# Turning beta, kappa and v of an RWKV chunk with whole-array transposes

## Chip, core and metric

The kernel runs on one NeuronCore of one Trainium2 chip. The metric is the device time of one launch in microseconds. All times below are from executions on the chip.

## The reference

One block of a hybrid model over 256 tokens of width 2048. The normalised input is projected once; four branches (a gated linear recurrence, an attention with forgetting, an SSD scan and an RWKV-7 scan) work on parts of the projection, each result is multiplied by its own weights and its own gate, the sum goes through `w_out`, and a feed-forward stage and a gated embedding stage follow. Only the RWKV scan is touched here. Cut to it:

```python
def step(state, inp):                       # state: heads x 64 (v) x 64 (k)
    r_t, w_t, k_t, v_t, kk_t, a_t = inp
    sa = einsum('bhvk,bhk->bhv', state, -kk_t)
    state = (state * w_t[:, :, None, :] + sa[..., None] * (kk_t * a_t)[:, :, None, :]
             + v_t[..., None] * k_t[:, :, None, :])
    return state, einsum('bhvk,bhk->bhv', state, r_t)
```

There are 8 heads of 64 channels. Everything is float32.

## The kernel before

**The main stream.** Most of the work is a long row of projections with weights from HBM. Each weight piece (`wr`, 512 KB) is loaded by a DMA on the SP queue, split by ScalarE into a rounded part (`wh`, L212) and by VectorE into the rest (`wl`, L213), and TensorE multiplies each part with activations that are split in the same way (`x`, or `sb` and others), into PSUM tiles `pg` (pool `psG`, 4 banks). In the profile these are the rows `pg<-x,wh`, `pg<-x,wl` and `pg<-sb,wh` of L132. There are 4 buffers for `wr` and 3 each for `wh` and `wl`.

**The branches beside it.** Each branch is a generator (`lru`, `ssd`, `fox`, `rwkv`). After each few matmuls of a projection the function `pump` may run one step of the branch at the head of the list, up to its next `yield`; a small credit (`RATE` 0.5 for each call, at least `STEP` 0.2 spent for each step) keeps it from running ahead. Instructions of a branch have a lower priority than the main stream, but its TensorE instructions get the place of the main stream's current one plus `DELAY` (16) (`on_pe`, recorded as L135). From this a planner, which works with a simulated time, writes down one order of instructions for each engine, and each engine executes its own in order. The branches' PSUM tiles are `pb` (pool `psB`, 4 banks, taken with `bank()`). The order of the merge is: recurrence, SSD, attention, RWKV; the RWKV result is needed only when its own product with `w_branch` begins, after all the gates of its turn.

**RWKV.** The 256 tokens are four chunks of 64, and the heads stand in four pairs `j`: two heads share the 128 partitions, head h in partitions 64h to 64h+63 (`H2[h]`). For each chunk `c` a DMA brings `jc`, of shape [128 partitions, 4 pairs, 8 kinds, 64], in a buffer `e`. The kinds that matter here are 1 (beta), 2 (kappa) and 3 (v); in memory they are neighbours, 64 columns each, with kind 0 before kind 1. The partitions of kinds 1 to 3 are channels and their columns tokens; the products of the scan need them with tokens in the partitions. So three "turns" stand at the head of a chunk: `vc`, `btk` and `ktk` (the last two only for chunks 0 to 2, since the last chunk hands on no state).

A turn is `heads([(jc[:, :, k], ident)])`: for each pair and each head, a 64x64 block is turned into its place of a PSUM bank. Head 0 uses TensorE's transpose; head 1, whose block lies in partitions 64 to 127, is multiplied by the unit matrix `ident`, which lies in the constants `cbr`. `kept` then copies the 128x256 result to SBUF with ScalarE (L956). In the profile the rows of the turns on TensorE are `pb<-cbr,e`. After the turns come `uu`, `sa`, the new state `pS` and the output `py`, products of 64x64 blocks by the same `heads`. A `yield` stands behind each turn.

Lines that matter: 132 and 135 (the calls that record a matmul of the main stream and of a branch), 172 (`bank`), 937 to 951 (`heads`), 953 to 959 (`kept`), 960 to 966 (the turns), 968 to 986 (the rest of a chunk).

Of the kernel before, what the change touches and what calls it, by code (L numbers as in the profile page):

```python
# [14 lines left out]
P = 128  # L15
# [70 lines left out]
def body(tc, T, out, dbg=None):  # L86
    nc = tc.nc
    V, A, G, PE = nc.vector, nc.scalar, nc.gpsimd, nc.tensor
# [13 lines left out]
    def mul(o, a, b):  # L102
        tt(o, a, b, ALU.mult)

    def add(o, a, b):
        tt(o, a, b, ALU.add)
# [19 lines left out]
    def act(o, i, f, **kw):  # L126
        A.activation(o, i, f, **kw)  # L127


    def on_pe(f, *a, **kw):  # L130
        if cur[0] != "b":
            return f(*a, **kw)  # L132
        p = tc.cur_priority
        tc.cur_priority = prio["m"] + DELAY
        f(*a, **kw)  # L135
        tc.cur_priority = p

    def mm(o, l, r, start=True, stop=True):
        on_pe(PE.matmul, o, l, r, start=start, stop=stop)

    def transpose(o, i, e):
        on_pe(PE.transpose, o, i, e)
# [25 lines left out]
    def slot(dt=F32, pool=sp):  # L168
        return pool.tile([P, S], dt, name="sb" if pool is not sp else "s", tag="s")

    def bank():
        return psB.tile([P, 512], F32, name="pb", tag="pb")
# [9 lines left out]
    def bslot(dt=F32):  # L182
        return slot(dt, bp)
# [244 lines left out]
    def eslot(shape):  # L428
        return bc_.tile(shape, F32, name="e", tag="e", bufs=3)
# [4 lines left out]
    def cc(name):  # L434
        o, n = CONST_OFF[name]
        return cbr[:, o:o + n]
# [4 lines left out]
    ident = cc("ident")  # L441
# [12 lines left out]
    H2 = [slice(0, 64), slice(64, 128)]  # L454
# [318 lines left out]
    def rwkv():  # L773
# [4 lines left out]
        for i in range(14):  # L778
            o = bslot()
# [8 lines left out]
        pt = bank()  # L788
# [19 lines left out]
        for j in range(4):  # L808
# [31 lines left out]
            b = bslot()  # L840
# [88 lines left out]
        j4 = "p (j v) -> p j v"  # L929
        S0 = None  # L930
        for c in range(4):
            ct = slice(c * 64, c * 64 + 64)

            jc = eslot([P, 4, 8, 64])
            dq.dma_start(jc, J[:, :, c, 0:8])
            rho, mr, mk, al, mak = [jc[:, :, i] for i in (0, 4, 5, 6, 7)]
            def heads(terms, pt=None):


                pt = bank() if pt is None else pt  # L940
                for j in range(4):
                    for i, (l, r) in enumerate(terms):
                        for h in (1, 0):
                            hs = H2[h]
                            o = pt[hs, j * 64:j * 64 + 64]
                            if h == 0 and r is ident:
                                transpose(o, l[hs, j], ident[hs, hs])
                                continue
                            mm(o, l[hs, j], r[hs, j] if r is not ident else ident[hs, hs],
                               start=i == 0, stop=i == len(terms) - 1)  # L950
                return pt[:, :S]

            def kept(pt, scale=1.0):
                o = bslot()
                if scale == 1.0:
                    A.copy(o, pt)  # L956
                else:
                    act(o, pt, AF.Copy, scale=scale)
                return o.rearrange(j4, j=4)
            vc = kept(heads([(jc[:, :, 3], ident)]))  # L960
            yield
            if c < 3:
                btk = kept(heads([(jc[:, :, 1], ident)]))
                yield
                ktk = kept(heads([(jc[:, :, 2], ident)]))
                yield
            qc = qbd.rearrange("p (j c) v -> p j c v", c=4)[:, :, c]
            uu = kept(heads(([(al, S0)] if S0 is not None else []) + [(mak, vc)]))
            yield
            sa = kept(heads([(qc, uu)]), -1.0)  # L970
            yield
            if c < 3:
                pS = heads([(btk, sa), (ktk, vc)])
            py = heads([(vc, mk)] + ([(S0, rho)] if S0 is not None else []) + [(sa, mr)])
            A.copy(yT[:, :, ct], py.rearrange("p (j t) -> p j t", j=4))
            if c < 3:
                S1 = bslot()
                pe_c = pend[:, :, c].unsqueeze(2).broadcast_to([P, 4, 64])
                S1v = S1.rearrange(j4, j=4)
                if S0 is None:  # L980
                    mul(S1v, pS.rearrange(j4, j=4), pe_c)
                else:
                    add(S1v, pS.rearrange(j4, j=4), S0)
                    mul(S1v, S1v, pe_c)
                S0 = S1v
            yield
# [3 lines left out]
        for j in range(4):  # L990
            pt = bank()
            mm2(pt[:, :S], center, yT[:, j], pool=bp)
            o = bslot()
# [105 lines left out]
    launch("b", fox)  # L1099
    proj("du", 12, 7)  # L1100
    launch("d", rwkv)


# [83 lines left out]
    acc1, hs = [None], []  # L1187
# [144 lines left out]
```

## Time and profile before

| | |
|---|---|
| median of 3 runs | 1761.89 us (1750.37 to 1765.18) |
| the profiled execution | 1751.44 us, span of its instructions 1749.6 us |
| mean granted TensorE clock | 0.995 |
| TensorE busy | 1730.1 us, 99% of the span |
| VectorE, ScalarE, GpSimd busy | 1237.7, 942.9, 102.8 us |
| DMA | 336.27 MB, mean 192 GB/s |

How to read the rows: engines are PE (TensorE's matmuls), PEld (its weight loads, beside the matmuls), DVE (VectorE), ACT (ScalarE), POOL (GpSimd) and SP. A group's row has the line, the engine, the operation, `out<-in` by the program's names, the array's shape for a matmul (rows*columns of the stationary operand), the shape of the moving operand, the count, then busy time and mean duration in ns, then the engine's idle time before these instructions and what ended it. A row of the order of time has start, duration, engine, line, operation, names, shape and count; the duration covers all that were merged, and matmuls overlap, so what one costs is read from start to start. A row of waits has who waited for whom, the total, how often, and the longest. A row of windows has the stretch, its length, then for PE, PEld, DVE, ACT and POOL the busy time and the count, then the granted clock of TensorE (1.00 is full), the DMA engines' busy share and GB/s.

### The profile page before, as it was taken

What the parts mean: (1) busy time and instruction counts of PE and PEld (TensorE: products, weight loads), DVE (VectorE), ACT (ScalarE), POOL (GpSimd) and SP (SyncE); (2) the same over time, 40 slices, a digit from 0 to 9 for tenths busy, and PEclk for the clock granted to TensorE, in tenths of its full rate; (3) what the DMA queues carried; (4) which work ended last, traced back from release to release, by engine and by line L of the source; (5) the groups of instructions that cost most, each with busy time, mean ns of one, the idle gap of its engine ahead of it and who ended that gap; (6) DMA issues with size and microseconds to landing.
All of it is one profiled execution on the core that took longest, in us unless ns stands there. A gap on an engine that the chain in (4) does not pass through costs nothing.

```text
span 1749.6 us, 29736 instructions
## 1 busy us (share of the span) xinstructions
PE 1730.1 (99%) x11621; PEld 1567.8 (90%) x11621; DVE 1237.7 (71%) x1998; ACT 942.9 (54%) x1422; POOL 102.8 (6%) x160
## 2 busy tenths in 40 slices
PE   8999999999999999999999999999999999999998
PEld 6888888999999989999888888888888888888887
DVE  7788767677789732668678777777777765555666
ACT  6586445556644433545556555555555544444554
POOL 4000000002320100000110000000000000000000
PEclk9999999999999999999999999999999999999999
DMA  7555556556675743565776666656666666656573
GB/s 265 172 178 188 180 174 214 188 183 207 205 214 175 248 137 118 175 198 185 237 227 188 189 190 192 191 186 190 192 189 197 214 208 189 193 190 191 171 227 133
DMA packets 98844, 336.27 MB, mean 192 GB/s; under 512 B 12330, under 2 KB 16592, under 8 KB 98704
## 3 DMA queue, kind: packets, MB, share of 16 engines
q1 hardware_dynamic: 90528, 310.94, 56.3%
q0 software_dynamic: 7456, 21.81, 4.3%
q8 instruction: 91, 1.49, 0.4%
q10 hardware_dynamic: 720, 1.63, 0.3%
q14 instruction: 49, 0.40, 0.1%
HBM read 324.85 MB, written 9.48 MB: 191 GB/s over the span
## 4 chain that ended last, share of the span: by engine, by line
PE 82%; DVE 1%; DMA 0%; issue 0%; ACT 0%; POOLq 0%
PE pg L132 78%; PE pb L135 4%; PE pb L132 1%; DMA e<-fox_rn 0%; DVE wl L213 0%; DVE sb L100 0%; DVE sb L120 0%; DVE s L100 0%; DMA fox_rn<-sb 0%; ACT s L253 0%; POOLq L466 0%
## 5 line engine op out<-in xcount | busy, mean ns | idle before, releaser
L132 PE MATMUL pg<-x,wh 128*128 128x512 f32 (+1 forms) x4384 | 1172.3, 340 | 3.4 <-DVE sb L100 2.7
L213 DVE TENSOR_TENSOR wl<-wr,wh 128x1024 fp32r<-128x1024 f32 (+1 forms) x592 | 716.9, 1212 | 419.6 <-ACT wh L212 412.6
L212 ACT CAST wh<-wr 128x1024 fp32r<-128x1024 f32 (+1 forms) x592 | 615.4, 1041 | 645.7 <-PE pg L132 503.3
L132 PE MATMUL pg<-x,wl 128*128 128x256 f32 (+1 forms) x3344 | 919.7, 283 | 8.8 <-DVE wl L213 8.8
L132 PEld LDWEIGHTS pg<-x,wh 128*128 128x128 f32 x4384 | 748.0, 188 | 89.8 <-issue 4.0
L132 PEld LDWEIGHTS pg<-x,wl 128*128 128x128 f32 (+1 forms) x3344 | 630.4, 189 | 23.7 <-DVE wl L213 11.6
L132 PE MATMUL pg<-f,wh 128*128 128x512 f32 x704 | 243.2, 391 | 0.0
L132 PE MATMUL pg<-f,wl 128*128 128x256 f32 x704 | 195.8, 282 | 0.0
L132 PEld LDWEIGHTS pg<-f,wh 128*128 128x128 f32 x704 | 131.7, 188 | 26.9
L132 PEld LDWEIGHTS pg<-f,wl 128*128 128x128 f32 x704 | 133.2, 189 | 1.0
L132 PE MATMUL pg<-sb,wh 128*128 128x256 f32 x512 | 93.8, 282 | 0.0
L120 DVE SCALAR_TENSOR_TENSOR s<-s,prm 128x255 f32<-128x255 f32 (+1 forms) x176 | 84.0, 477 | 1.7 <-ACT s L127 1.0
L132 PEld LDWEIGHTS pg<-sb,wh 128*128 128x128 f32 x512 | 79.0, 189 | 0.3
L253 ACT COPY s<-pg 128x256 f32<-128x256 f32 x136 | 49.5, 365 | 44.7 <-PE pg L132 44.7
L132 PE MATMUL pg<-sb,wl 128*128 128x256 f32 x256 | 72.6, 285 | 0.0
L100 DVE TENSOR_TENSOR s<-s 128x256 f32<-128x256 f32 (+1 forms) x172 | 70.6, 420 | 1.4
L127 ACT ACTIVATE s<-s 128x256 f32<-128x256 f32 x140 | 56.4, 411 | 17.0 <-DVE s L100 16.7
L100 DVE TENSOR_TENSOR s<-s,pg 128x256 f32<-128x256 f32 x136 | 56.2, 414 | 9.3 <-ACT s L253 8.1
L127 ACT ACTIVATE s<-s,prm 128x256 f32<-128x256 f32 x88 | 52.4, 596 | 0.8 <-DVE s L100 0.8
L127 ACT ACT_TABLE_LOAD x39 | 50.0, 1283 | 1.9 <-PEq L1322 1.2
L132 PEld LDWEIGHTS pg<-sb,wl 128*128 128x128 f32 x256 | 48.3, 189 | 0.3
L132 PE MATMUL pg<-e,wh 128*128 128x512 f32 x128 | 44.9, 391 | 0.0
(232 smaller groups left out, 1189.3 us busy)
## 6 DMA issues: line engine op xcount, KB each, us to landing
wr<-in_w_up_dram SPq DMA_DIRECT2D x176, 512.0 KB, 4.3
wr<-in_w_g_dram SPq DMA_DIRECT2D x128, 512.0 KB, 3.8
wr<-in_w_down_dram SPq DMA_DIRECT2D x88, 512.0 KB, 4.2
wr<-in_w_p_dram SPq DMA_DIRECT2D x76, 512.0 KB, 3.8
wr<-in_w_branch_dram SPq DMA_DIRECT2D x32, 512.0 KB, 3.7
wr<-in_w_out_dram SPq DMA_DIRECT2D x32, 512.0 KB, 3.9
wr<-in_w_ple_gate_dram SPq DMA_DIRECT2D x32, 512.0 KB, 4.7
wr<-in_w_v_dram SPq DMA_DIRECT2D x8, 512.0 KB, 4.2
```

Source lines behind the costliest of these rows:

```text
L100: V.tensor_tensor(o, a, b, op=op)
L120: V.scalar_tensor_tensor(o, a, s, b, op0=op0, op1=op1)
L127: A.activation(o, i, f, **kw)
L132: return f(*a, **kw)
L135: f(*a, **kw)
L212: A.copy(wh, wr)
L213: V.tensor_tensor(wl, wr, wh.bitcast(F32), op=ALU.subtract)
L253: A.copy(o, pt[:, S:])
```

## The change

The products with the unit matrix and the 64x64 transposes go. In their place TensorE's transpose turns two neighbouring kinds of a pair at once: a block of 128 partitions (two heads) and 128 columns (kinds k and k+1). Of the result, partitions 0 to 63 are kind k's tokens and partitions 64 to 127 kind k+1's, each with both heads side by side in the columns. Head 0 of kind k is right in the lower half, head 1 of kind k+1 in the upper half, and these are copied; the other two quarters are not used. So each kind is needed twice, once as the first and once as the second of two neighbours: the loop goes over k = 3 (alone, 64 columns), 2 (with 3), 1 (with 2) and 0 (with 1) in chunks 0 to 2, and over 3 and 2 in the last. Each pass takes a bank, does four transposes, one or two copies of 64 partitions on ScalarE, and a `yield`.

```diff
@@ heads
-                            if h == 0 and r is ident:
-                                transpose(o, l[hs, j], ident[hs, hs])
-                                continue
-                            mm(o, l[hs, j], r[hs, j] if r is not ident else ident[hs, hs],
-                               start=i == 0, stop=i == len(terms) - 1)
+                            mm(o, l[hs, j], r[hs, j], start=i == 0, stop=i == len(terms) - 1)
@@ the head of a chunk
-            vc = kept(heads([(jc[:, :, 3], ident)]))
-            yield
+            tk = {k: bslot().rearrange(j4, j=4) for k in ((1, 2, 3) if c < 3 else (3,))}
+            for k in (3, 2, 1, 0):
+                if k not in tk and k + 1 not in tk:
+                    continue
+                pt = bank()
+                n = 2 if k + 1 in tk else 1
+                for j in range(4):
+                    transpose(pt[:n * 64, j * P:j * P + P], jc[:, j, k:k + n].rearrange("p a b -> p (a b)"), ident)
+                for h in range(n):
+                    if k + h in tk:
+                        A.copy(tk[k + h][H2[h]],
+                               pt[H2[h]].rearrange("p (j h v) -> p j h v", j=4, h=2)[:, :, h])
+                yield
+            vc = tk[3]
             if c < 3:
-                btk = kept(heads([(jc[:, :, 1], ident)]))
-                yield
-                ktk = kept(heads([(jc[:, :, 2], ident)]))
-                yield
+                btk, ktk = tk[1], tk[2]
```

## The prediction

> **What bounds the kernel now.** I read the page first: the span, the engines' busy times and the chain that ended last.
>
> ```profile
> span 1749.6 us, 29736 instructions
> PE 1730.1 (99%) x11621; PEld 1567.8 (90%) x11621; DVE 1237.7 (71%) x1998; ACT 942.9 (54%) x1422; POOL 102.8 (6%) x160
> ...
> PE 82%; DVE 1%; DMA 0%; issue 0%; ACT 0%; POOLq 0%
> ```
>
> TensorE is busy for 1730.1 of 1749.6 us, and the chain runs along it. A busy share alone can deceive, since the ends of matmuls are modelled; so next I asked whom TensorE waits for, over the whole span and then from 600 to 800 us, where the RWKV chunks run.
>
> ```profile
> PE pg L132 <- DVE wl L213: 8.8, 8, 2.9
> ...
> PE pg L132 <- DVE sb L100: 0.3, 1, 0.3
> ```
>
> The first row is the largest wait of the whole span, 8.8 us over eight times; the second is all that TensorE waits between 600 and 800 us: 0.3 us. So in the stage of the change TensorE is an unbroken queue, and what is taken out of its queue should come off the end. Then I asked for the groups of TensorE's instructions by form, and read the turns of k, beta and v (moving operand `cbr`, the constants, with the unit matrix; stationary operand `e`, which is `jc`).
>
> ```profile
> L135 PE MATMUL pb<-cbr,e 64*64 64x64 f32 x120 | 18.1, 247 | 0.0
> L135 PE MATMUL pb<-cbr,sb 128*128 128x128 f32 x22 | 4.7, 272 | 0.0
> ```
>
> The first row is what the change replaces. Ten turns (three in each of chunks 0 to 2, one in chunk 3) issue 8 instructions each, 80 in all; the trace has 120 records, because an fp32 product shows as two records and a transpose as one: 40 x 2 + 40 = 120. They hold TensorE for 18.1 us, 0.15 us a record. The second row is the form that comes in, a whole 128x128 transpose, as the SSD and attention branches already use it.
>
> Last, the order of time around chunk 1's turns, and the granted clock there.
>
> ```profile
> 644.34 0.40 PE L132 MATMUL pg<-sb,wh 128*128 128x256 f32 x2
> 644.67 5.62 PE L135 MATMUL pb<-cbr,e 64*64 64x64 f32 x36
> 650.22 0.48 PE L135 MATMUL pb<-sb,e 64*64 64x64 f32 x4
> 650.63 0.58 PE L132 MATMUL pg<-sb,wl 128*128 128x256 f32 x1
> ...
> 652.29 0.63 PE L132 MATMUL pg<-x,wh 128*128 128x256 f32 x2
> 652.72 0.42 PE L132 MATMUL pg<-x,wl 128*128 128x256 f32 x1
> ```
>
> ```profile
> 645.59:649.00 3.41, 3.41 (x26) 2.34 (x25) 0.00 (x0) 0.74 (x2) 0.00 (x0) 1.00 0.56 160
> 649.00:652.41 3.41, 3.41 (x19) 2.82 (x19) 0.42 (x1) 1.06 (x2) 0.00 (x0) 0.50 0.00 0
> 652.41:655.83 3.42, 3.42 (x38) 3.08 (x36) 1.61 (x2) 0.35 (x1) 0.00 (x0) 0.50 0.25 53
> 655.83:659.24 3.41, 3.41 (x41) 3.27 (x39) 0.58 (x1) 1.42 (x2) 0.00 (x0) 1.00 0.26 101
> ...
> 666.07:669.48 3.41, 3.41 (x26) 2.35 (x24) 0.00 (x0) 0.74 (x2) 0.90 (x2) 1.00 0.85 269
> 669.48:672.89 3.41, 3.41 (x18) 2.87 (x17) 0.00 (x0) 0.37 (x1) 0.00 (x0) 0.50 0.41 153
> 672.89:676.31 3.42, 3.42 (x36) 3.08 (x37) 1.23 (x1) 1.42 (x2) 0.00 (x0) 0.50 0.00 0
> 676.31:679.72 3.41, 3.41 (x40) 3.21 (x40) 0.42 (x1) 1.14 (x2) 0.00 (x0) 1.00 0.51 154
> ```
>
> This is the less visible cost. In chunk 1 the three turns stand in one block of 36 records. At 649.00, 4.3 us after the block begins, the granted clock (the column after POOL's) falls to 0.50, and it stays there until 655.83, well after the block is over: the projection matmuls that follow start 0.43 / 2 = 0.215 us apart (652.29 to 652.72, two of them). Chunk 2 does the same from 669.48 to 676.31.
>
> **The change, part by part.** *The pairs go.* Taken out: 18.1 us of TensorE's queue.
>
> *Whole transposes come in.* A bank of four transposes for each of the kinds 3, 2, 1, 0 in chunks 0 to 2, and for 3 and 2 in chunk 3: 3 x 16 + 8 = 56, each one record. Their price comes from where the attention branch mixes three of them with projection matmuls:
>
> ```profile
> 333.93 0.28 PE L132 MATMUL pg<-x,wh 128*128 128x256 f32 x1
> 334.05 0.28 PE L132 MATMUL pg<-x,wl 128*128 128x256 f32 x1
> 334.16 0.40 PE L132 MATMUL pg<-x,wh 128*128 128x256 f32 x2
> 334.40 0.28 PE L132 MATMUL pg<-x,wl 128*128 128x256 f32 x1
> 334.52 0.27 PE L135 MATMUL pb<-cbr,sb 128*128 128x128 f32 x1
> 334.55 0.37 PE L132 MATMUL pg<-x,wh 128*128 128x256 f32 x1
> 334.75 0.38 PE L135 MATMUL pb<-cbr,sb 128*128 128x128 f32 x2
> 334.89 0.37 PE L132 MATMUL pg<-x,wh 128*128 128x256 f32 x1
> 335.09 0.28 PE L132 MATMUL pg<-x,wl 128*128 128x256 f32 x1
> ```
>
> From 333.93 to 334.40 four projection matmuls start, 0.117 us each. From 334.40 to 335.09 pass 0.69 us with three of them (0.35) and three transposes: 0.34 / 3 = 0.114 us a transpose, entry and exit included. 56 x 0.114 = 6.4 us. Sixteen of the 56 (kind 3 alone) turn 64 columns instead of 128, a form that the trace does not show. From below, they cost half, 16 x 0.057 = 0.9 us less; from above, each bank of four pays for a change of the array's shape like the pairs, 0.15 us a record, 16 x 0.036 = 0.6 us more. I take 0.114, the nearest row. [...]
>
> So the queue is shorter by 18.1 - 6.4 = 11.7 us (11.1 to 12.6).
>
> *The half clock goes.* The blocks of 36 records become at most 16 x 0.114 = 1.8 us long. That so much is harmless is seen at chunk 0, where the turns lie apart:
>
> ```profile
> 618.28:621.69 3.41, 1.85 (x13) 1.17 (x13) 0.00 (x0) 0.60 (x2) 1.00 0.05 22
> ```
>
> ```profile
> 620.00:630.00 10.00, 10.00 (x81) 8.00 (x80) 4.38 (x7) 3.27 (x6) 0.00 (x0) 1.00 0.17 54
> 630.00:644.70 14.70, 14.70 (x181) 14.16 (x179) 6.18 (x8) 5.57 (x8) 0.75 (x1) 1.00 0.65 206
> ```
>
> The first row counts TensorE's records into `pb` alone: 1.85 of 3.41 us were pairs; the two others count everything, and the clock stays at 1.00. At half clock a projection matmul took 0.215 us for 0.117, so 1 - 0.117 / 0.215 = 46% of such time is lost. Outside the blocks themselves, whose slowed records are in the 18.1 already, that is 655.83 - 650.22 = 5.6 us after chunk 1 and 676.31 less the block's end after chunk 2:
>
> ```profile
> 664.63 5.24 PE L135 MATMUL pb<-cbr,e 64*64 64x64 f32 x36
> 669.80 0.79 PE L132 MATMUL pg<-x,wh 128*128 128x256 f32 x2
> ```
>
> 676.31 - 669.80 = 6.5 us. Together 12.1 x 0.46 = 5.6 us. The drop came 4.3 us into one block and 4.85 us (664.63 to 669.48) into the other, so it isn't at a fixed distance; blocks of 5.5 and 5.2 us may in other executions end before it. For the median of runs I therefore count two thirds, 3.7 us (0 to 5.6).
>
> *ScalarE's copies double.* Ten copies of 128x256 become twenty of 64x256 (six in chunks 0 to 2, two in chunk 3).
>
> ```profile
> L956 ACT COPY sb<-pb 128x256 f32<-128x256 f32 x14 | 5.2, 372 | 23.7 <-PE pb L135 23.7
> L862 ACT COPY beb<-d 64x256 f32<-64x256 f32 x8 | 3.2, 405 | 0.1
> ```
>
> Half the partitions save nothing (405 ns from SBUF, against 372 from PSUM): ten more copies are 3.7 to 4.1 us on ScalarE. ScalarE is idle for nearly half the span, and before these very copies it waits 23.7 us for TensorE; that covers them. If the cover were gone, weight casts (`wh`) queue behind the copies and TensorE waits for them, by at most those 4.1 us.
>
> *Banks and waits.* Fourteen banks of the four in `psB` are used for turns instead of ten. TensorE executes in order, so a transpose that waits for a bank holds all projections behind it; a bank is free once ScalarE has read it. A group of four takes 0.46 us and its two copies 0.75: in a run of four groups TensorE gets ahead of ScalarE by about 0.3 us a group, and the fourth group can meet a bank that the chunk before still holds (`pS`, `py`). I set 1.0 us for all chunks (0 to 4).
>
> *Four more yields.* One more stop of the generator per chunk moves the rest of RWKV back by about one step of the projections each, 12 matmuls x 0.117 = 1.4 us, 5.6 us in all. It has room:
>
> ```profile
> 750.29 0.41 ACT L218 CAST sb<-sb 128x256 fp32r<-128x256 f32 x1 [0.26 <-DVE sb L100]
> ...
> 797.85 0.40 PE L132 MATMUL pg<-sb,wh 128*128 128x256 f32 x2
> ```
>
> RWKV's last output is cast at 750.7 us, and the branch product that first reads it starts at 797.85: 47 us. Cost nothing; without that cover, 5.6 us. No DMA is added or moved.
>
> **The sum.** Against the profiled execution's own time, 1751.44 us: -11.7 - 5.6 + 1.0 = -16.3, hence 1735. That execution lies 10.4 us below the median of the runs shown, 1761.89 (1750.37 to 1765.18). Against the median: -11.7 - 3.7 + 1.0 = -14.4, hence **1747.5 us**, 0.8% less. With the terms' bounds the case runs from 1761.89 - 12.6 - 5.6 = 1743.7 to 1761.89 - 11.1 + 4 = 1754.8, and since the runs before spread by 14.8 us I widen its low end to 1738.
>
> **Rivals.** *The half clock stays.* The pairs hold two products for each transpose; the new blocks hold no product at all, and in chunk 2 they follow directly on small 64x64 products. If transposes pass for idleness, 1.8 us of them with such neighbours may suffice for a drop. Then only the queue's 11.7 less 1.0 is won on an execution with both drops: 1751; with one drop more (5.6 / 2 = 2.8 us each) 1754. For it: what sets the drop off is not told by rows. Against it: the row of 618.28, and the blocks are a third as long. [...]
>
> *Nothing arrives.* The order of all instructions is planned anew, and the time freed could turn into waits for split weights (`wl`, 8.8 us now) or be lost in another order later. Against it: TensorE's 0.3 us of waits between 600 and 800. It gives 1762.
>
> *Slower.* TensorE stalls on the banks at each of the fourteen groups: ScalarE, in order, may have a weight cast ahead of the two copies, and TensorE stands meanwhile.
>
> ```profile
> L212 ACT CAST wh<-wr 128x1024 fp32r<-128x1024 f32 x578 | 606.8, 1051 | 628.3 <-PE pg L132 489.3 <-issue 69.0 <-ACT s L253 21.6
> ```
>
> Price: 1.05 + 2 x 0.37 = 1.8, less the group's own 0.46, 1.3 us; 14 x 1.3 = 18.8 in place of the 1.0, so -11.7 - 3.7 + 18.8 = +3.4: 1765. It decides from 15.4 / 14 = 1.1 us a group on. Against it: there are four banks, and now ScalarE waits for TensorE there, not the reverse.
>
> **How the numbers follow.** Forecast 0.60 at 1747.5; half clock stays 0.23 (1751 to 1754); nothing arrives 0.10 (1762); slower 0.07 (1765). The range 1737 to 1760 takes in the first two and leaves the others out. About 1% is what a measurement of this kernel can tell from no change: 17.6 us. The forecast lies 3.2 us short of it, so of its 0.60 and the second case's 0.23 I give 0.30 to faster by over 1%; 0.04 to slower by over 1%, for which the stall would need 2.4 us a group; 0.66 to within 1%.
>
> **What would show it.** In the profile after: 56 records `pb<-cbr,e` with 128 moving columns, some 6.4 us busy instead of 18.1; granted clock 1.00 from 600 to 700 us; twenty 64x256 copies of `sb<-pb` near 0.37 us; TensorE's waits on `psB` readers under 2 us. The prediction is wrong if a half clock stands behind the transposes, if a transposing group costs well over 0.46 us, or if waits of TensorE elsewhere grow by several us.

## The result, and the profile after

The changed kernel takes 1735.42 us (median of 4 runs, 1734.35 to 1737.99) against 1760.96 for the kernel before (4 runs, 1750.37 to 1765.18): a ratio of 0.9866, 95% interval 0.9821 to 0.9911. That is 1.3% faster. Forecast were 1747.5 and a range of 1737 to 1760; the measured median lies 1.6 us below the range. The profiled executions, 1751.44 and 1737.99 us, differ by 13.4 us only. So there are two things to explain: the stage of the chunks, and why the medians are farther apart than the profiles.

The page after the change, its span and its busy times:

```profile
span 1736.2 us, 29617 instructions
PE 1714.4 (99%) x11557; PEld 1557.9 (90%) x11557; DVE 1238.4 (71%) x1998; ACT 946.8 (55%) x1432; POOL 103.0 (6%) x160
```

TensorE's busy time fell by 15.7 us and the span by 13.4: the bound is where it was. The groups of the turns from 590 to 720 us on TensorE, and of their copies on ScalarE:

```profile
L135 PE MATMUL pb<-cbr,e 128*128 128x128 f32 x40 | 6.0, 272 | 0.0
L135 PE MATMUL pb<-cbr,e 128*64 128x128 f32 x16 | 2.5, 278 | 0.0
...
L968 ACT COPY sb<-pb 64x256 f32<-64x256 f32 x20 | 7.1, 367 | 1.7 <-PE pb L135 1.3
```

The 56 transposes are there, 8.5 us busy where the pairs had 18.1 (busy times of matmuls overlap the neighbours': a whole transpose's record lasts 272 ns and the next starts 109 ns after it, so the net is less; it comes below). ScalarE's twenty copies take 367 ns each, and it hardly waits for TensorE before them. The block of chunk 1 in the order of time, and the granted clock over the whole stage:

```profile
644.62 1.91 PE L135 MATMUL pb<-cbr,e 128*64 128x128 f32 x16
```

```profile
600.00:700.00 100.00, 100.00 (x1234) 96.25 (x1233) 45.89 (x65) 44.45 (x78) 3.59 (x6) 1.00 0.55 175
```

36 records in 5.62 us have become 16 in 1.91, and both half-clock stretches are gone: 1.00 over the 100 us.

To compare the stage in all kernels I use the main stream, which is the same in each: 10518 records into `pg`. The table has the starts of the 3751st and the 4501st of them in each profile (before, 592.65 and 729.18 us), which enclose all four chunks.

| profile | 3751st, 4501st (us) | between | against before |
|---|---|---|---|
| before | 592.65, 729.18 | 136.53 | |
| after | 595.45, 714.87 | 119.42 | -17.1 |
| after, again (c0) | 591.80, 711.16 | 119.36 | -17.2 |
| all products (e1) | 598.13, 717.39 | 119.26 | -17.3 |
| grouped (e2) | 594.60, 719.49 | 124.89 | -11.6 |
| transposes three times (e3) | 595.89, 727.67 | 131.78 | -4.8 |
| new in chunks 0, 3 (e4) | 595.29, 727.06 | 131.77 | -4.8 |
| new in chunks 1, 2 (e5) | 592.17, 716.27 | 124.10 | -12.4 |
| old in chunk 0 alone (e7) | 593.12, 716.54 | 123.42 | -13.1 |
| products three times (e6) | 594.80, 722.34 | 127.54 | -9.0 |
| before, three further ones (b1, b2, b3) | | 136.30, 136.04, 136.24 | -0.2 to -0.5 |
| before, a fourth (b4) | 594.38, 739.02 | 144.64 | +8.1 |

The stage gained 17.1 us, the forecast's 11.7 + 5.6 = 17.3. Of that the profiled execution shows 13.4 in its span: before the stage it was 2.8 us behind. Of these, 2.5 us were lost at 170 us, far from the change, by a longer wait (0.9 us more) and by a half clock that the profile of before did not have there (3.41 us of it, of which 46% or 1.6 us is lost):

```profile
166.50:170.00 3.50, 0.37 (x2) 0.37 (x2) 3.50 (x13) 3.49 (x9) 0.00 (x0) 0.95 0.01 2
170.00:173.40 3.40, 3.40 (x13) 2.87 (x13) 3.40 (x7) 1.36 (x3) 0.00 (x0) 0.55 0.51 154
```

TensorE works 0.37 us of the first stretch, since it waits for split weights there (3.8 us; 2.9 us in the profile of before), and the clock falls afterwards. Another 0.9 us is given back between 715 and 746 us; waits account for 0.4 of it, the rest was not followed up.

### The profile page after: what moved, and what is told of

Its sections match the earlier page's. It is cut to its first block, busy times and chain, and to the rows that moved or that the text cites. A ratio compares the mean times of both kernels' runs of the same rounds, so it can differ in the third digit from the quotient of the medians.

```text
span 1736.2 us, 29617 instructions
## 1 busy us (share of the span) xinstructions
PE 1714.4 (99%) x11557; PEld 1557.9 (90%) x11557; DVE 1238.4 (71%) x1998; ACT 946.8 (55%) x1432; POOL 103.0 (6%) x160
## 4 chain that ended last, share of the span: by engine, by line
PE 71%; issue 8%; DVE 2%; DMA 1%; POOL 0%; ACT 0%; POOLq 0%; DVEq 0%
PE pg L132 69%; PE pb L135 1%; DVE wl L213 1%; PE pb L132 1%; DMA e<-fox_rn 0%; DMA d<-rw_gn 0%; DMA rw_q<-e 0%; DVE e L100 0%; DVE e L896 0%; DVE s L100 0%; DVE sb L120 0%; DVE sb L100 0%; DMA rw_gn<-sb 0%; POOL qbd L911 0%; POOL e L935 0%
```

## The experiments

My theory was that of the prediction: a shorter queue, and two half-clock stretches fewer. Rivals: a gain of the new order, or another cost within the pairs.

**The changed kernel beside the kernel before (c0).**

> The changed kernel beside the kernel before on one chip, as the yardstick of the others. My theory: the stage from 590 to 700 us is shorter by 17 us (11.7 from a shorter TensorE queue, 5.6 from two half-clock stretches that are gone), and everything else differs only by chance, so in executions of the kernel before that are near 1762 there must be more half clock elsewhere, to be seen as a lower granted clock of those executions. Rival: the rest of the difference of the medians (25 us against 17) is a gain of the new order of instructions; then the changed kernel is ahead by about 25 us also of executions whose granted clock is as high as that of the profiled one.

Measured: 1735.61 us (1733.76 to 1736.51, 5 runs) against 1756.36 (16 runs), ratio 0.9873 (0.9844 to 0.9902). Each run of the kernel before also has its granted clock. In this and the two later sets there are 46: 23 with 0.993 to 0.995, at 1750.02 to 1756.29 us, median 1752.2; and 23 with 0.987 to 0.990, at 1756.43 to 1765.78, median 1760.2. The changed kernel's nine executions have 0.997 to 0.999 and a median of 1735.6. Against the first half it is ahead by 16.6 us, about the stage's 17.1; the rest is a matter of the clock, as the theory had it, and the rival falls.

**All products (e1).**

```diff
-                            if h == 0 and r is ident:
-                                transpose(o, l[hs, j], ident[hs, hs])
-                                continue
```

> The loop of before, with head 0 multiplied by the unit matrix as well: no transpose at all, ten copies, no more yields. If it is the alternation of a product and a transpose in each pair that costs 0.43 us, sixteen records of a turn should run like the sixteen of sa, some 0.5 us with 0.2 for entry and exit: 10 turns x 0.7 = 7 us in place of 18.1, blocks of at most 1.7 us, no half clock, and a time equal to the changed kernel's within 3 us. If fp32 products with the unit matrix are themselves the slow part, the 120 records become 160 and the time goes up, 18.1 x 160/120 = 24 us, some 1767.

```profile
L135 PE MATMUL pb<-cbr,e 64*64 64x64 f32 x160 | 6.6, 221 | 0.0
```

160 records in 6.6 us, in place of 120 in 18.1. Time 1735.49 us (1733.76 to 1740.4, 6 runs), ratio 0.988 (0.9852 to 0.9908); stage -17.3. Taking three lines away from the kernel before does what the whole change does. So whole transposes were not needed for the gain: the 0.43 us a pair goes with the transposes between the products. Turning from head 1 to head 0 is not what costs, since the products of e1 do that too. Whether it is the transposes themselves or their taking turns with products, the next run tells.

**Grouped (e2).** The same 120 records, head 1's four products first and then head 0's four transposes.

```diff
+                if terms[0][1] is ident:
+                    l = terms[0][0]
+                    for j in range(4):
+                        mm(pt[H2[1], j * 64:j * 64 + 64], l[H2[1], j], ident[H2[1], H2[1]])
+                    for j in range(4):
+                        transpose(pt[H2[0], j * 64:j * 64 + 64], l[H2[0], j], ident[H2[0], H2[0]])
+                    return pt[:, :S]
```

> The loop of before in another order: the four products of head 1 first, then the four transposes of head 0. The same 120 records. If alternation costs: one change of kind in a turn in place of seven; eight product records of 0.06 and four transposes of 0.11 with 0.2 around, 1.1 us in place of 1.7, 11 to 12 us in all, blocks of 3.3 us at the edge of a half clock: 6 to 12 us faster than before. If each transpose of 64x64 is slow by itself: no change from before, 18.1 us and both half-clock stretches.

```profile
L135 PE MATMUL pb<-cbr,e 64*64 64x64 f32 x120 | 10.2, 224 | 0.0
```

```profile
644.60 2.91 PE L135 MATMUL pb<-cbr,e 64*64 64x64 f32 x36
```

```profile
644.49:647.90 3.41, 3.41 (x43) 2.76 (x42) 0.80 (x3) 1.10 (x3) 0.00 (x0) 1.00 0.56 184
647.90:651.31 3.41, 3.41 (x31) 3.18 (x32) 2.03 (x3) 1.06 (x2) 0.00 (x0) 0.50 0.02 6
```

10.2 us for the same records, transposes among them: a product and a transpose in turn is what cost eight of the 18 us. Time 1740.45 us (6 runs), ratio 0.9901 (0.9873 to 0.993). In the stretch from 644.49 to 647.90 stand 0.3 us of projections, the block of 2.91 us and two small products of `uu`; a half clock of 3.41 us followed it, and behind the like block of chunk 2 there was none. So of two blocks of 2.9 us the clock fell behind one; that 3.3 us would be "at the edge" was my estimate, and no run sets a limit.

**Transposes three times (e3).**

```diff
-                for j in range(4):
+                for j in [q // 3 for q in range(12)]:
                     transpose(pt[:n * 64, j * P:j * P + P], ...)
```

> The changed kernel with each of its 56 transposes issued three times in a row: 112 more of 0.109 us, 12.2 us. In chunks 1 and 2 they make blocks of 48, 5.2 us long, as long as the blocks of pairs before. If whole transposes keep the clock up (they fill the array): 12.2 us slower than the changed kernel, granted clock 1.00 there. If transposes do not count as work for the clock, as the rival had it: a half clock about 4 to 5 us into each block, 12.2 + 5 to 6 = 18 us slower.

```profile
648.55 5.40 PE L135 MATMUL pb<-cbr,e 128*64 128x128 f32 x48
```

```profile
645.00:650.40 5.40, 5.40 (x49) 5.40 (x48) 4.21 (x7) 3.03 (x5) 0.00 (x0) 1.00 0.72 267
650.40:660.00 9.60, 9.60 (x117) 9.16 (x116) 1.23 (x1) 3.67 (x9) 0.00 (x0) 1.00 0.19 57
```

48 transposes and nothing else for 5.2 us, and the clock stays at 1.00, as it does over the like block of chunk 2 (from 663.89 on). The stage is 12.4 us longer than the changed kernel's (12.2 expected without a half clock); the time 1747.87 us (11 runs), ratio 0.995 (0.9932 to 0.9969). Whole transposes cost 12.4 / 112 = 0.11 us each, and over both blocks of them (5.40 and 5.43 us) the clock was 1.00.

**The chunks apart (e4, e5).** In each, the new head for the named chunks and the old one for the others:

```diff
+            if c in (0, 3):        # e5: (1, 2)
+                ...                # the loop of whole transposes
+            else:
                 vc = kept(heads([(jc[:, :, 3], ident)]))
                 ...
```

> Whole transposes in chunks 0 and 3 alone, the old pairs in chunks 1 and 2, whose 36-record blocks stay. My theory: the queue of chunks 0 and 3 shrinks from 7.4 us (1.7 + 2.0 + 2.0 + 1.7) to 24 x 0.109 = 2.6, 4.8 us faster; the half-clock stretches behind chunks 1 and 2 stay, and with them the spread of the executions, from a granted clock of 0.995 down to 0.987: a median of 4 to 6 us below the kernel before, some executions 10 us above the best. Rival (the gain of the medians is one of order and not of the clock): the spread goes as well and the median falls by 10 us or more.

> Whole transposes in chunks 1 and 2 alone. My theory: 10.7 us of blocks become 32 x 0.109 = 3.5, 7.2 us; no half clock between 600 and 700 us; so 12.8 us on an execution like the profiled one of before, and the spread goes: all executions within 4 us, granted clock 0.997 or higher, a median of 1740. Rival: if the extra half clock of the slower executions comes from chunk 0 or from elsewhere, some executions stay near 1750.

Stage: -4.8 and -12.4, as expected (-4.8, -12.8); together -17.2, so the two parts add up. Clock in the profiles, from 640 to 680 us, first e4, then e5:

```profile
640.00:680.00 40.00, 40.00 (x392) 34.66 (x391) 11.62 (x18) 11.75 (x21) 1.83 (x3) 0.83 0.39 132
```

```profile
640.00:680.00 40.00, 40.00 (x532) 37.50 (x531) 16.59 (x25) 17.12 (x33) 1.83 (x3) 1.00 0.50 161
```

But I had the spread the wrong way round. e4, with the long blocks left in, ran 1746.65 to 1752.2 us, median 1749.8, at a clock of 0.992 to 0.995 (10 runs, ratio 0.9951, 0.993 to 0.9972): the clock of 0.987 to 0.990 was gone. e5, without them, ran 1739.2 to 1750.24, median 1745.33 in place of the 1740 expected, at 0.992 to 0.998 (6 runs, ratio 0.9924, 0.9894 to 0.9953). The extra half clock does not come from the blocks of chunks 1 and 2.

**Chunk 0 alone (e7), and profiles of the kernel before (b1 to b4).** e7 is e4 with `if c in (1, 2, 3)`.

> The old pairs in chunk 0 alone, whole transposes in chunks 1 to 3. With the pairs kept in chunks 0 and 3 (the run named e5) executions spread over 11 us and the granted clock went down to 0.992; with them kept in chunks 1 and 2 (e4) it did not go below 0.992 from 0.995. If the spread comes from chunk 0, where 2 us of 64x32 products stand directly ahead of the first turn and two more turns follow within 9 us, this kernel spreads as e5 did: its best execution at 1737.5 (5.7 - 16 x 0.109 = 4.0 us over the changed kernel's best), others up to 11 us more. If it comes from chunk 3, all executions lie within 4 us of 1737.5 to 1739 with a clock of 0.997 or more.

> The kernel before unchanged, for another profile. Of 16 executions, seven had a granted clock of 0.994 to 0.995 and nine 0.987 to 0.993. My theory: in one of 0.987 to 0.990 the half clock lasts some 25 us longer in all, and it stands in the stage of the chunks, behind the blocks of 36 records, costing some 10 us there. Rival: it stands elsewhere, at the start or near 170 us where TensorE waits for split weights.

> The same once more, since each execution falls by chance on a high or a low granted clock: as for the profile ahead of it.

> The kernel before once more for its profile: 18 of 33 executions so far had a granted clock of 0.992 or less, but the three that left a profile had 0.994 to 0.995. If this one is of the others, its extra half clock stands around chunk 0, from 615 to 640 us; rival: behind chunks 1 to 3.

> The same, for the same reason: a second chance for a profile of an execution with the lower granted clock.

e7: best 1738.44, median 1745.61, others up to 1752.08 us at clocks from 0.999 down to 0.990 (10 runs, ratio 0.995, 0.9929 to 0.997). So chunk 0's pairs alone bring the spread. The profiles of e5 and e7 are of executions with a high clock (0.998 and 0.999), so they don't show where the lost clock of the others stands. b1, b2 and b3 took 1753.78, 1752.15 and 1752.21 us at 0.994 and showed the two stretches behind chunks 1 and 2 as the first profile did, and none at chunk 0. b4 took 1761.4 us at 0.988, and has one there. Windows of b4, first the one at 170 us, with its half clock, then those of chunk 0:

```profile
170.13:173.55 3.42, 3.42 (x12) 2.95 (x13) 3.42 (x8) 1.59 (x4) 0.00 (x0) 0.50 0.46 153
```

```profile
617.28:620.69 3.41, 3.41 (x75) 2.87 (x71) 0.27 (x1) 1.59 (x3) 0.00 (x0) 1.00 0.49 181
620.69:624.11 3.42, 3.42 (x14) 2.76 (x14) 1.40 (x2) 1.74 (x3) 0.00 (x0) 0.50 0.02 6
624.11:641.17 17.06, 17.06 (x84) 14.29 (x84) 3.12 (x6) 2.66 (x5) 0.00 (x0) 0.50 0.20 62
641.17:644.58 3.41, 3.41 (x40) 3.21 (x39) 1.23 (x1) 0.94 (x3) 0.00 (x0) 1.00 0.21 29
```

A half clock from 620.69 to 641.17, 20.5 us. It lowers the mean over 1760 us by 0.5 x 20.5 / 1760 = 0.006, which is just what sets 0.988 apart from 0.994. Its order of time, and then that of the first profile of before at the same place:

```profile
617.02 2.06 PE L135 MATMUL pb<-qbd,xt 64*64 64x32 f32 x64
618.91 1.76 PE L135 MATMUL pb<-cbr,e 64*64 64x64 f32 x12
620.60 0.74 PE L132 MATMUL pg<-x,wh 128*128 128x256 f32 x2
```

```profile
615.22 2.06 PE L135 MATMUL pb<-qbd,xt 64*64 64x32 f32 x64
...
617.11 1.76 PE L135 MATMUL pb<-cbr,e 64*64 64x64 f32 x12
```

```profile
614.87:618.28 3.41, 3.41 (x77) 2.94 (x75) 0.88 (x2) 1.37 (x3) 0.00 (x0) 1.00 0.67 223
618.28:621.69 3.41, 3.41 (x24) 2.60 (x24) 1.30 (x2) 1.96 (x4) 0.00 (x0) 1.00 0.05 22
```

Both executions issue the same: 64 records of 64x32 and then the first turn's twelve, 3.58 us in a row (617.02 to 620.60). What differs is how that row lies to the times at which the granted clock changes. Within a profile these lie on one grid, with steps of 3.413 us: in the first profile 649.00, 655.83, 669.48 and 676.31 are 2, 4 and 2 steps apart; in b4 the drop at 620.69 lies 450.56 us, 132 steps, behind the one at 170.13. In b4 the row covers a stretch of this grid all but for 0.1 us; in the first profile the nearest stretch, 614.87 to 618.28, begins with 0.35 us of projections, and the clock stays. The other five profiles with the old chunk 0 (b1 to b3, e5 and e7) have at least 0.45 us of projections in each such stretch, and no drop there. The drop cost b4 8.1 us in the stage. With a new first turn of four transposes the row is 2.0 + 0.4 us (618.09 to 620.46 in the profile after), shorter than a stretch, and all nine executions of the changed kernel had a clock of 0.997 or more.

That the phase decides is read from these seven profiles, one of them with the drop; no run moved the phase on purpose. And a stretch without projections is neither enough for a drop nor needed for one. The first profile of before has one that holds 2.0 us of 64x64 products of the scan and 1.4 us of pairs, counted from start to start, at full clock before and after:

```profile
662.65:666.07 3.42, 3.42 (x86) 3.00 (x82) 1.68 (x3) 0.37 (x1) 0.93 (x2) 1.00 0.47 129
```

In b2 the block of chunk 1 began 0.8 us into its stretch (at 646.38, in 645.58 to 649.00), and the clock fell at 649.00 all the same. What the stretch must hold is open.

**Products three times (e6).** e1 with each product with the unit matrix issued three times:

```diff
-                for j in range(4):
+                for j in ([q // 3 for q in range(12)] if terms[0][1] is ident else range(4)):
```

> The all-products kernel (e1) with each product with the unit matrix issued three times: 160 more instructions, 320 more records of 0.029 us, 9.3 us more. In chunks 1 and 2 they make blocks of 72 products, 4.2 us long. If it is the small part of the array at work that lets the clock fall (a product of 64x64 uses a quarter), a half clock stands behind these blocks, some 3 to 6 us each on top of the 9.3; if it is the transposes among the pairs, the clock stays at 1.00, and the time is e1's and 9.3 us.

```profile
646.82 4.41 PE L135 MATMUL pb<-cbr,e 64*64 64x64 f32 x144
```

```profile
650.40:660.00 9.60, 9.60 (x179) 9.20 (x175) 3.30 (x4) 3.23 (x5) 0.00 (x0) 1.00 0.20 61
```

One execution, 1745.35 us; 4.2 us of small products, and no half clock behind them. The stage is 8.3 us longer than e1's (9.3 expected). So over 4.2 us of small products of two heads, issued 0.03 us apart, the clock stayed at 1.00 too; it fell during the slow pairs of chunks 1 and 2 (blocks of 5.6 and 5.2 us) and behind one of e2's two half-and-half blocks (2.9 us). Both hold 64x64 transposes. No run has a long row of these alone, so whether the slow issue or the 64x64 transposes let the clock fall is not told apart.

## Why the prediction was right, and where it was not

*The queue.* Right: 17.3 us were forecast for the profiled execution's stage, queue and clock together; measured 17.1. By e4, where the clock is not in play, 24 transposes replaced the pairs of two chunks for -4.8 against -4.8.

*The narrow transposes.* The middle value held: chunk 1's sixteen, four of them narrow, took 1.91 us in all, and the last one's end is in it; narrow and whole ones start 0.109 us apart alike. Half the price, the lower bound, was not seen: with 64 columns on the stationary side and, as in the others, 128 on the moving one they took as long. The upper bound's price for a change of the array's shape, 0.15 us a record, no run shows: from the last narrow transpose to the first whole one (644.945 to 645.054 us) pass 0.109 us, as between any two in the row.

*The half clock of chunks 1 and 2.* Right that both stretches go, and right in size. The reason given, that the new blocks are short, is not the whole of it: e3's blocks are as long as the old ones (5.4 us against 5.6 and 5.2) and the clock stayed at 1.00, so what stands in a block counts too. The rival, that whole transposes pass for idleness, is refuted by e3: 5.2 us of fp32 transposes and nothing else, with the clock at 1.00 ahead of them, over them and behind them. Whether they could bring a half clock back up no run here shows.

*The step that failed* is the half-clock term for the median, "two thirds, 3.7 us (0 to 5.6)". I argued that in other executions the drop might miss, so that the gain would be smaller. In all five profiles of the kernel before, and in e4's, both drops are there, and in each the block took 2.6 us or more of one stretch of the clock's grid. And I took one row, the 1.85 us of pairs at 618.28 without a drop, to show that chunk 0 is harmless. It was one execution: b4 lost its clock at chunk 0 too, for 20.5 us, at 8.1 us in the stage. That this happens in half of the executions is inferred: 23 of 46 have b4's clock and time, and their median lies 8.0 us above the others'. The term should then have been 5.6 + 0.5 x 8.1 = 9.7 us in the mean. The median of before that I started from, 1761.89, belongs by its time to the executions with that stretch: 1761.89 - 11.7 - 5.6 - 8.1 = 1736.5, where 1735.42 was measured. The spread of 14.8 us in the runs shown was the sign of it, and I used it only to widen the range (whose low end stands as 1738 in one place of the prediction and as 1737 in another; the measured median lies below both). The chances went wrong with the term: 0.66 was on a change within 1%, 0.30 on faster by over 1%, and the ratio is 0.9866.

*Banks and waits.* 1.0 us (0 to 4) was set; TensorE shows no wait from 590 to 720 us. In chunks 0, 2 and 3 projections stand between the groups, and even chunk 1's four groups in a row met no bank in use. The slower rival has nothing for it, and the rival by which nothing arrives falls with the stage's 17.1 us.

*Copies and yields.* Right: 367 ns a copy, hidden. RWKV's last cast is at 736.9 us and its first use at 784.4, 47 us as before.

## What to carry to other kernels

When TensorE is the bound, count a small operation by its start-to-start time in its real neighbourhood: a product and a transpose in turn cost 0.43 us a pair (before, start to start: 0.106 + 0.150 + 0.172), while products in a row cost 0.03 us a record (e6) and whole transposes 0.11 (e3). Look at the granted clock behind every such run, and in more than one profile: at each row of slow pairs of over 5 us it fell in all six profiles that have them, behind e2's two rows of 2.9 us it fell once, and behind chunk 0's row of 3.6 us in one of seven profiles. So a spread of the runs with a spread of their granted clocks can itself be a cost, and here it was one that could be removed. Here three lines less, products alone, did as much as the whole rewrite.

## What was not expected of the hardware

The half clock lasted longer than the row ahead of it: one step of 3.413 us behind e2's block, two (6.83 us) behind the blocks of chunks 1 and 2, six (20.5 us) in b4. In b4 chunk 0's two other turns fell into that time, twelve records each, and so did the 16 records of `uu`; the six steps end at 641.17:

```profile
622.97 0.47 PE L135 MATMUL pb<-cbr,e 64*64 64x64 f32 x2
623.89 2.23 PE L135 MATMUL pb<-cbr,e 64*64 64x64 f32 x10
...
628.70 0.47 PE L135 MATMUL pb<-cbr,e 64*64 64x64 f32 x2
629.61 2.23 PE L135 MATMUL pb<-cbr,e 64*64 64x64 f32 x10
...
635.34 1.11 PE L135 MATMUL pb<-sb,e 64*64 64x64 f32 x14
```

Only the sixth step, from 637.76 on, holds projections alone. But that is not needed for the end: behind chunk 1 in the first profile the last half-clock step, 652.41 to 655.83, has 28 records of small products in it (1.7 us). What sets the length is open; no run here varied it.

And TensorE was not idle when the clock fell in these stretches (busy throughout in e2's and b4's rows), nor did small work as such bring it about: 144 records of 64x64 in 4.2 us kept the clock at 1.00, and with 36 records in 5.6 us (before) or in 2.9 us (e2) it fell. Whether slow issue or the 64x64 transposes among the 36 are the cause is open, as said above. In b4 it fell behind a mixture: 64 records of 64x32, issued as closely as e6's (0.03 us apart), and one turn of pairs.
